# Softmax numerators of the first block in SBUF, and their low fp16 half on GpSimd

## The chip, the cores and the metric

The kernel runs on one core of a Trainium2 chip. The metric is the device time of one launch, in microseconds (us). The core has five engines that work through queues of their own, in order: TensorE (PE, with PEld for its weight loads), VectorE (DVE), ScalarE (ACT), GpSimd (POOL) and SyncE (SP, which here only issues DMAs).

## What is computed

The first block is two layers over 512 latent tokens and, in the first layer, 256 context tokens as well. Each layer adds three gated branches: a Fourier branch, a neighbourhood attention (NA, 8 heads of 64) and a latent attention (MLA, 8 heads of 96), then a layer norm and a gated feed-forward. A second block follows (sliding-window and forgetting attention, a recurrent unit, 16 experts). The attentions of the first block all have this form:

```
for each layer l in (0, 1):                   # "last" in layer 1: no context queries
    NA :  P = exp(q k^T / 8 + bias - max);  y = (P v) / sum(P)     # 256 window keys + 256 context keys
    MLA:  P = exp(q k^T / sqrt(96) - max);  y = (P v) / sum(P)     # 768 keys
    context queries (layer 0 only): the same over the 256 context keys
```

Matmuls are to be float32-accurate, so every operand is kept as a pair of fp16 numbers, a high half and a low half (the low half is the value less the high half), and each product is three matmuls: high by high, high by low, low by high.

## The kernel before

**Units.** The attentions run as units, one for a tile of 128 queries. An NA unit (`na_unit`) takes a pair of heads at 512 keys each, so a tile of numerators of 128 x 1024; a context unit (`ctx_unit`) a pair of heads at 256 keys, 128 x 512; an MLA unit (`mla_head`) one head at 768 keys, 128 x 768. Layer 0 has four pairs of 4 NA units and 2 context units, then four pairs of 8 MLA units and 2 context units; layer 1 the same without the context units. So there are 32 units of 128 x 1024, 64 of 128 x 768 and 16 of 128 x 512, in four stages: NA and MLA of layer 0, NA and MLA of layer 1.

**Steps of a unit.** The scores S are six or twelve matmuls into one of three PSUM buffers of 128 x 1024 (`big()`, pool `ps2`), which every projection of the kernel uses too. DVE takes the maximum of each row (L904, or L871 and L874) and scales it (L906, L877); ACT writes exp(S) back over S in PSUM, with its row sums (L908, L881). Then `turn_rows`: ACT copies the numerators to fp16 (L766, the high half), DVE subtracts that from the numerators in PSUM (L767, the low half), both into a tile p16 with two buffers, and two DMAs on SP's queue turn the halves into ph (L769; three buffers). PE multiplies ph by v (L152, L154, L156: the first two use the high half of ph, L156 the low half), DVE divides by the sums (L786, L788), PE transposes (L794), and ACT and DVE make the pair of fp16 halves (L161, L162).

**Order.** `pipeline` emits the stages of consecutive units overlapped: the scores of unit u, `turn_rows` of u - 1, the product with v of u - 4 (u - 2 in NA). Between them come "fills": the projections that make q, k and v of the next pair (`na_prep`, `mla_prep`), and the gated projections of the branch before (`branch`), whose weights are loaded by SP into a staging tile and split by ACT (L124) and DVE (L129, both inputs in SBUF) into a pair in pool `w16`. The framework's scheduler then fixes one order of instructions per engine, by a model of its own.

**GpSimd** has little to do in these stages: it adds the gated branches up (L638), scales the bias of NA (L843), and issues the DMAs of the shifted v, the bias and of part of k (L839 to L842, L1011). All of its inputs here lie in SBUF.

Of the kernel before, what the change touches and what calls it, by code (L numbers as in the profile page):

```python
# [9 lines left out]
F32 = mybir.dt.float32  # L10
# [47 lines left out]
class Net:  # L58
    def __init__(self, ctx, tc, I, out):
# [6 lines left out]
        # staging, hi/lo and modulation weight buffers  # L66
        self.wst = ent(tc.tile_pool(name="wst", bufs=4))
        self.w16 = ent(tc.tile_pool(name="w16", bufs=8))
# [6 lines left out]
    def open_x(self):  # L75
        """Residual tiles; their pool sits on the other side of SBUF until close_x()."""
# [44 lines left out]
    # ---------------------------------------------------------------- helpers  # L121
# [23 lines left out]
    def mm3(self, outs, lhs, rhs, first=True, last=True):  # L145
        """outs[j] += lhs[k].T @ rhs[j][k]; every operand is a (hi, lo) pair."""
# [11 lines left out]
    def hilo(self, dst, src, scale):  # L158
        """dst[:, 0/1] (fp16) = hi/lo of scale * src."""
# [4 lines left out]
    def rsqrt(self, v, shape, pool, tag):  # L164
        """1/sqrt(v) for v > 0, float32-accurate; returns a new tile."""
# [11 lines left out]
    def token_rsqrt(self, sqs, nt, scale, eps, pool):  # L177
        """1/sqrt(scale * (mean over 256 features of sqs) + eps) of every token: a function that puts it on all
        partitions, in PSUM."""
# [19 lines left out]
    def dense(self, w, act, kts, chunks, m, first=True, last=True, outs=None):  # L199
        """w: (p, 2, k, c); act: list of (p, 2, k, T) per chunk."""  # L200
# [4 lines left out]
    def dense_early(self, ws, ctx, outs):  # L205
        """dense over all tokens with each of the weights, a chunk of tokens at a time."""
# [5 lines left out]
    # ------------------------------------------------------------ modulation  # L212
# [16 lines left out]
    def modvec(self, w_ap, cols, bias, mod):  # L229
        """Generator of small steps: mod (p, 48, len(cols)) = columns of silu(c) @ w_mod + b_mod, feature  # L230
        128 * index + p."""
        nc = self.nc
        for g in range(3):
            row = self.sm.tile([128, 512], F32, tag="mrow", name="mrow", bufs=1)
            for kt in range(KD):
                # the first third, whose steps follow one another, adds up in PSUM
# [19 lines left out]
    def modvec_sums(self, w_ap, cols, bias, mod, new, keep={}):  # L256
        """As modvec, with the sums over kt on the vector engine."""
# [54 lines left out]
    def pump(self, n=1):  # L312
        """Emit up to n steps of the background work."""
        while n and self.bg is not None:
            if next(self.bg, self) is self:
                self.bg = None
            n -= 1
# [5 lines left out]
    def affine(self, name, g, b, mod, i_shift, i_scale, nm):  # L323
        """(g, b) of a norm followed by x * (1 + scale) + shift, times AS: (p, 8, nm) each."""
# [29 lines left out]
    # ------------------------------------------------------------ layer norms  # L354
# [34 lines left out]
    def stats(self, x, t0, n, g=None, gb=None):  # L389
        """PSUM tile, on all partitions: mean over features of x in [:, :n], of x^2 in [:, n:2n]; with g and  # L390
        gb, of x * gb and (x * g)^2."""
# [18 lines left out]
    def ln_chunk(self, x, t0, n, apply, between=None):  # L410
        """In place: x[:, :, t0:t0+n] <- (x - mean) * rstd, then apply()."""
# [1824 lines left out]
```

## Time and profile before

| | before |
|---|---|
| time, median of 3 runs | 2865.58 us (2861.57, 2865.58, 2868.97) |
| span of the profiled execution | 2860.5 us |
| PE busy | 2571.4 us, 90% |
| DVE busy | 1787.7 us, 62% |
| ACT busy | 1130.4 us, 40% |
| POOL busy | 277.3 us, 10% |

The span runs from the first to the last instruction; what lies around it is some us more (the three times are 1.1 to 8.5 us above the span, 5.1 us at the median). The page has no time of the profiled execution itself, only this span. The shares are averages over stages with different limits, so the four attention stages have to be read one by one: 126 to 335 us (NA, layer 0), 400 to 635 us (MLA, layer 0), 1423 to 1584 us (NA, layer 1) and 1632 to 1814 us (MLA, layer 1).

### The profile page before, as it was taken

Reading aid. Unit: us, or ns where it says so; the run is one execution under the profiler, and the core shown is the slowest. Engines: PE = TensorE matmul, PEld = TensorE weight load, DVE = VectorE, ACT = ScalarE, POOL = GpSimd, SP = SyncE. Lnnn points to the kernel's source line nnn. Section 1 sums busy time; section 2 is a strip of 40 time slices with the busy share of each in tenths; the row PEclk is TensorE's granted clock in tenths of the full one; section 3 lists DMA queues with packets and bytes.
Section 4 is the critical chain, followed back from the end, with each engine's and each line's share of the span. In section 5 each row is a group of like instructions: output and inputs, shape, how many; then the busy total and the mean of one; then the engine's idle time right before and its main releaser. Section 6 shows DMA issues by size and latency. Waiting matters only on the chain. (4 is left out here: it accounts for less than half of the span.)

```text
span 2860.5 us, 45500 instructions
## 1 busy us (share of the span) xinstructions
PE 2571.4 (90%) x18514; PEld 1537.5 (54%) x18514; DVE 1787.7 (62%) x3041; ACT 1130.4 (40%) x1876; POOL 277.3 (10%) x229
## 2 busy tenths in 40 slices
PE   6999988899999999999998888999999887886784
PEld 4766555556675555556665444466444444543342
DVE  7555586653375656364655767547565477879895
ACT  4444344443342122123644355434222244544562
POOL 4100000011000000000000000100000000013552
PEclk9999899999999999999998989999999998877997
DMA  9366546683034535251455267525665603646883
GB/s 313 94 150 134 114 112 135 138 189 98 23 94 128 148 97 150 76 158 39 132 130 127 70 120 144 134 60 161 200 185 160 174 16 74 138 133 217 273 286 115
DMA packets 561674, 389.13 MB, mean 136 GB/s; under 512 B 229644, under 2 KB 524108, under 8 KB 561200
## 3 DMA queue, kind: packets, MB, share of 16 engines
q1 hardware_dynamic: 547568, 344.75, 46.0%
q0 software_dynamic: 13024, 38.24, 4.2%
q8 instruction: 147, 2.41, 0.3%
q10 hardware_dynamic: 864, 3.15, 0.3%
q14 instruction: 71, 0.58, 0.1%
HBM read 316.29 MB, written 23.62 MB: 119 GB/s over the span
## 5 line engine op out<-in xcount | busy, mean ns | idle before, releaser
L152 PE MATMUL ps<-aL,w 128*128 128x512 f16 (+1 forms) x1504 | 541.1, 361 | 16.1 <-DVE p L767 10.6
L154 PE MATMUL ps<-aL,w 128*128 128x512 f16 (+1 forms) x1504 | 541.4, 360 | 1.1 <-DVE aL L444 1.0
L156 PE MATMUL ps<-aL,w 128*128 128x512 f16 (+1 forms) x1504 | 540.6, 360 | 0.0
L124 ACT ACTIVATE w<-wst 128x1024 f16<-128x1024 f32 (+2 forms) x333 | 340.1, 1023 | 461.0 <-PE ps L156 412.6
L129 DVE SCALAR_TENSOR_TENSOR w<-wst,w 128x1024 f16<-128x1024 f32 (+2 forms) x326 | 400.4, 1232 | 161.3 <-ACT w L124 159.3
L152 PEld LDWEIGHTS <-w 128*128 128x128 f16 (+1 forms) x3276 | 323.4, 99 | 286.9 <-issue 49.6
L156 PEld LDWEIGHTS <-w 128*128 128x128 f16 (+1 forms) x3276 | 324.2, 99 | 255.7 <-issue 40.1
L154 PEld LDWEIGHTS <-w 128*128 128x128 f16 (+1 forms) x3276 | 324.9, 99 | 236.4 <-issue 25.9
L154 PE MATMUL ps<-aC,w 128*128 128x256 f16 (+1 forms) x720 | 196.4, 273 | 0.8 <-DVE aC L444 0.7
L152 PE MATMUL ps<-aC,w 128*128 128x256 f16 (+1 forms) x720 | 196.1, 273 | 1.1 <-ACT aC L443 1.1
L156 PE MATMUL ps<-aC,w 128*128 128x256 f16 (+1 forms) x720 | 196.3, 273 | 0.0
L278 DVE SCALAR_TENSOR_TENSOR mv<-wmod,csilu,mv 128x1024 f32<-128x1024 f32 x126 | 158.4, 1280 | 35.0 <-DMA wmod<-in_w_mod 34.6
L767 DVE TENSOR_TENSOR p<-ps,p 128x768 f16<-128x768 f32 (+2 forms) x126 | 125.9, 1001 | 76.9 <-ACT p L766 76.2
L766 ACT ACTIVATE p<-ps 128x768 f16<-128x768 f32 (+2 forms) x126 | 106.5, 848 | 31.1 <-DMA ph<-p 28.7
L152 PE MATMUL ps<-h,w 128*128 128x512 f16 (+1 forms) x384 | 111.4, 344 | 0.8 <-ACT h L1117 0.8
L154 PE MATMUL ps<-h,w 128*128 128x512 f16 (+1 forms) x384 | 111.3, 344 | 0.7 <-DVE h L1118 0.7
L156 PE MATMUL ps<-h,w 128*128 128x512 f16 (+1 forms) x384 | 111.3, 344 | 0.0
L638 POOL TENSOR_TENSOR acc<-acc,gt 128x768 f32<-128x768 f32 (+1 forms) x32 | 54.3, 1696 | 505.8 <-DVE gt L637 443.0
L908 ACT ACTIVATE ps<-ps,nm 128x768 f32<-128x768 f32 (+1 forms) x96 | 70.1, 730 | 76.0 <-DVE nm L906 70.1
L1113 ACT ACTIVATE ft<-ps 128x768 f32<-128x768 f32 (+1 forms) x44 | 30.9, 702 | 173.4 <-PE ps L156 173.3
L152 PEld LDWEIGHTS <-ph 128*128 128x128 f16 x800 | 78.2, 104 | 37.3 <-DMA ph<-p 23.1
L904 DVE TENSOR_REDUCE mx<-ps 128x1 f32<-128x768 f32 (+1 forms) x80 | 71.6, 898 | 42.2 <-PE ps L156 41.4
(688 smaller groups left out, 5171.1 us busy)
## 6 DMA issues: line engine op xcount, KB each, us to landing
wmod<-in_w_mod SPq DMA_DIRECT2D x144, 512.0 KB, 4.5
wst<-in_w_in SPq DMA_DIRECT2D x101, 512.0 KB, 4.2
wst<-in_w_ffn_gate SPq DMA_DIRECT2D x44, 512.0 KB, 4.1
wst<-in_w_ffn_up SPq DMA_DIRECT2D x44, 512.0 KB, 3.9
wst<-in_w_ffn_down SPq DMA_DIRECT2D x44, 512.0 KB, 4.6
wst<-in_w_branch SPq DMA_DIRECT2D x24, 512.0 KB, 3.6
wst<-in_w_out SPq DMA_DIRECT2D x24, 512.0 KB, 3.7
wst<-in_w_gate SPq DMA_DIRECT2D x38, 256.0 KB, 4.3
```

Of the source, the lines that this page charges most:

```text
L124: nc.scalar.activation(w[:, HI], src, AF.Copy, scale=WS)
L129: nc.vector.scalar_tensor_tensor(w[:, LO], src, WS, w[:, HI], ALU.mult, ALU.subtract)
L152: mm(o, lhs[k][HI], rhs[j][k][HI], start=s, stop=False)
L154: mm(o, lhs[k][HI], rhs[j][k][LO], start=False, stop=False)
L156: self.last_mm = mm(o, lhs[k][LO], rhs[j][k][HI], start=False, stop=e)
L278: nc.vector.scalar_tensor_tensor(a, st, self.cs[:, kt, c:c + 1], a, ALU.mult, ALU.add)
L638: nc.gpsimd.tensor_tensor(self.acc[:, kt + 1], self.acc[:, kt + 1], t[:, :T], op=ALU.add)
L766: nc.scalar.activation(hi, P, AF.Copy)
L767: nc.vector.tensor_tensor(lo, P, hi, op=ALU.subtract)
L904: nc.vector.tensor_reduce(mx[:, :nh], Sv, AX.X, ALU.max)
L908: nc.scalar.activation(P[:, h], Sv[:, h], AF.Exp, scale=SC, bias=nm[:, h:h + 1], accum_out=sums[:, h:h + 1])
L1113: nc.scalar.activation(t, pg[:, :T], AF.Tanh, scale=0.5 * INV)
```

## The change

In the three kinds of units the exponential writes into a new SBUF tile p32 (two buffers) and no longer over the scores in PSUM. `turn_rows` then reads p32 twice: ACT makes the high half, and GpSimd, which is now passed as the engine, the low half. The sliding-window and forgetting attentions of the second block still call `turn_rows` without an engine and keep DVE. To make room for p32, pool `w16` has six buffers and not eight; in the expert stage a second pool gets six and not four, so both together stay at twelve there, and the experts and the last two tiles of the output projection's weights are handed out over the two pools accordingly. Beside this only comments go. Line numbers of the code behind `turn_rows` move by up to seven (L767 becomes L768, L638 stays, L908 becomes L913).

```diff
-        self.w16 = ent(tc.tile_pool(name="w16", bufs=8))
+        self.w16 = ent(tc.tile_pool(name="w16", bufs=6))
...
-    def turn_rows(self, pool, P, nh, ntile):
+    def turn_rows(self, pool, P, nh, ntile, eng=None):
+        eng = eng or nc.vector
...
-        nc.vector.tensor_tensor(lo, P, hi, op=ALU.subtract)
+        eng.tensor_tensor(lo, P, hi, op=ALU.subtract)
...
+    def rows32(self, pool, nh, n):
+        return pool.tile([128, nh * n], F32, tag="p32", name="p32", bufs=2).rearrange("p (h c) -> p h c", h=nh)
...
-        P = Sv
+        P = self.rows32(ap, 2, 512)
...
-        ph = self.turn_rows(ap, P, 2, 4)
+        ph = self.turn_rows(ap, P, 2, 4, self.nc.gpsimd)
...
-        P = S[:, None, :NT]
-        self.softmax_rows(ap, P, NT, SC, sums[:, h:h + 1], P)
+        P = self.rows32(ap, 1, NT)
+        self.softmax_rows(ap, S[:, None, :NT], NT, SC, sums[:, h:h + 1], P)
...
-        ph = self.turn_rows(ap, P, 1, 6)
+        ph = self.turn_rows(ap, P, 1, 6, self.nc.gpsimd)
...
+        spare = lambda: self.half[1].tile([128, 2, 1056], F16, tag="w16", name="w16")[:, :, None, :D]
...
-                tc.tile_pool(name="wxh", bufs=4, reuse_waits="tile") as x16:
+                tc.tile_pool(name="wxh", bufs=6, reuse_waits="tile") as x16:
```

The context units change as the NA units do, at 256 keys. Since a scheduler fixes the order, two places of it are shown.

DVE before, in MLA of layer 0, where the second pair's q is made (p16 with ps2 as its source is the low half of a unit, mx and nm the maximum and its scaled copy, krn and qh the rotation of q, w16 a split of weights):

```order
L906 TENSOR_SCALAR nm_5424<-mx_5422 128x1
L162 SCALAR_TENSOR_TENSOR yT_4087<-ps1_5493,yT_4087 128x128
L129 SCALAR_TENSOR_TENSOR w16_6421<-wst_6419,w16_6421 128x1024
L904 TENSOR_REDUCE mx_5482<-ps2_5475 128x1
L1058 TENSOR_TENSOR ps2_5453<-ps2_5453,ctab_91 32x512
L906 TENSOR_SCALAR nm_5484<-mx_5482 128x1
L767 TENSOR_TENSOR p16_5487<-ps2_5415,p16_5487 128x768
L1059 SCALAR_TENSOR_TENSOR krn_4093<-ps2_5453,ctab_91 32x512
```

DVE of the changed kernel at the same place (mx_5520 is the maximum that was mx_5482):

```order
L909 TENSOR_REDUCE mx_5520<-ps2_5512 128x1
L1063 TENSOR_TENSOR ps2_5490<-ps2_5490,ctab_91 32x512
L911 TENSOR_SCALAR nm_5522<-mx_5520 128x1
L129 SCALAR_TENSOR_TENSOR w16_6249<-wst_6247,w16_6249 128x1024
L1064 SCALAR_TENSOR_TENSOR krn_4117<-ps2_5490,ctab_91 32x512
L791 RECIPROCAL ri_5867<-sums_5450 128x2
```

The low half is gone from DVE's queue; the split of weights that stood ahead of the maximum now stands behind its scaled copy.

POOL before, in MLA of layer 0, from the second pair on (acc is the sum of the branches, kh the DMAs of a later pair's k):

```order
L638 TENSOR_TENSOR acc_454<-acc_454,gt_5572 128x768
L638 TENSOR_TENSOR acc_454<-acc_454,gt_5787 128x768
L1011 DMA kh_6003<-krn_4093 32x1536
L1011 DMA kh_6007<-krn_4093 32x1536
L638 TENSOR_TENSOR acc_454<-acc_454,gt_6258 128x768
```

POOL of the changed kernel at the same place:

```order
L768 TENSOR_TENSOR p16_5626<-p32_5519,p16_5626 128x768
L768 TENSOR_TENSOR p16_5694<-p32_5620,p16_5694 128x768
L638 TENSOR_TENSOR acc_454<-acc_454,gt_5610 128x768
L768 TENSOR_TENSOR p16_5746<-p32_5688,p16_5746 128x768
L768 TENSOR_TENSOR p16_5843<-p32_5740,p16_5843 128x768
L768 TENSOR_TENSOR p16_5913<-p32_5837,p16_5913 128x768
L638 TENSOR_TENSOR acc_454<-acc_454,gt_5828 128x768
L1016 DMA kh_6048<-krn_4117 32x1536
L768 TENSOR_TENSOR p16_5966<-p32_5906,p16_5966 128x512
```

Between two sums of branches there are now two to five low halves, and some low halves stand behind a sum or behind a DMA of kh.

## Rows read from the trace of the kernel before

**Rows 1.** Stages: us; busy PE, PEld, DVE, ACT, POOL; granted clock, DMA share, GB/s
```profile
126.00:335.00 209.00, 201.85 (x1962) 131.22 (x1960) 107.81 (x247) 89.06 (x180) 9.82 (x12) 0.95 0.63 136
...
400.00:635.00 235.00, 202.65 (x1771) 124.77 (x1770) 153.12 (x278) 114.09 (x216) 18.18 (x14) 0.95 0.70 144
...
1423.00:1584.00 161.00, 152.57 (x1476) 95.60 (x1475) 86.21 (x196) 70.76 (x135) 9.86 (x12) 0.95 0.59 132
...
1632.00:1814.00 182.00, 153.02 (x1210) 82.50 (x1209) 122.71 (x207) 96.64 (x163) 12.03 (x12) 0.90 0.66 124
```

**Rows 2.** PE's waits, 400 to 635 us: releaser, total us, times, longest
```profile
PE ps L152 <- DVE p L767: 11.5, 10, 3.6
...
PE ps L156 <- DMA ph<-p: 3.7, 8, 0.6
PE ps L152 <- DVE kh L162: 3.6, 2, 1.8
...
PE ps L152 <- DVE vm L162: 2.2, 2, 1.4
```

**Rows 3.** PE's waits, 1632 to 1814 us
```profile
PE ps L152 <- DVE p L767: 7.9, 4, 2.9
PE ps L156 <- DMA ph<-p: 5.9, 6, 2.2
...
PE ps L152 <- DVE vm L162: 2.8, 2, 1.8
...
PE ps L152 <- DVE kh L162: 2.2, 1, 2.2
```

**Rows 4.** PE's waits, 126 to 335 us
```profile
PE ps L156 <- DMA ph<-p: 2.4, 1, 2.4
...
PE ps L152 <- DVE p L767: 1.0, 1, 1.0
```

**Rows 5.** PE's waits, 1423 to 1584 us
```profile
PE ps L152 <- DVE p L767: 2.9, 2, 2.1
PE ps L156 <- DMA ph<-p: 1.0, 2, 0.6
```

**Rows 6.** Timeline around one stall of PE: start, us, instruction, idle before
```profile
475.42 0.86 ACT L908 ACTIVATE ps<-ps,nm 128x768 f32<-128x768 f32 x1
...
476.77 0.79 ACT L766 ACTIVATE p<-ps 128x768 f16<-128x768 f32 x1
...
478.60 0.96 DVE L767 TENSOR_TENSOR p<-ps,p 128x768 f16<-128x768 f32 x1
...
479.61 0.39 PE L152 MATMUL ps<-aL,w 128*128 128x512 f16 x1 [1.94 <-DVE p L767]
```

**Rows 7.** Groups by shape, DVE and ACT: count, busy us, mean ns, idle before
```profile
L129 DVE SCALAR_TENSOR_TENSOR w<-wst,w 128x1024 f16<-128x1024 f32 x306 | 388.3, 1273 | 141.3 <-ACT w L124 139.3
...
L767 DVE TENSOR_TENSOR p<-ps,p 128x768 f16<-128x768 f32 x66 | 62.8, 955 | 46.9 <-ACT p L766 46.4
...
L767 DVE TENSOR_TENSOR p<-ps,p 128x1024 f16<-128x1024 f32 x41 | 50.0, 1220 | 20.7 <-ACT p L766 20.6
...
L627 ACT ACTIVATE gt<-ps 128x768 f32<-128x768 f32 x24 | 19.4, 810 | 72.4 <-PE ps L156 72.4
```

**Rows 8.** The same view of POOL
```profile
L638 POOL TENSOR_TENSOR acc<-acc,gt 128x768 f32<-128x768 f32 x16 | 33.2, 2073 | 289.7 <-DVE gt L637 289.7
...
L127 POOL TENSOR_TENSOR w<-wst,w 128x1024 f16<-128x1024 f32 x7 | 16.2, 2319 | 0.6
```

**Rows 9.** Timeline of a DVE instruction beside one of POOL
```profile
449.52 1.80 POOL L638 TENSOR_TENSOR acc<-acc,gt 128x768 f32<-128x768 f32 x1 [14.20 <-DVE gt L637]
...
449.96 2.45 DVE L129 SCALAR_TENSOR_TENSOR w<-wst,w 128x1024 f16<-128x1024 f32 x1
```

**Rows 10.** The transposing DMAs (L769), from issue to landing
```profile
DMA to landing us min/median/max: 2.4/3.4/10.4
```

**Rows 11.** ACT's waits, 400 to 635 us
```profile
ACT p L766 <- DMA ph<-p: 14.6, 8, 4.3
```

More of the change, by code (lines that the diff above doesn't have):

```diff
@@ L923, in ctx_unit @@
         sums = ap.tile([128, 2], F32, tag="sums", name="sums", bufs=4)
-        P = Sv
+        P = self.rows32(ap, 2, 256)
         self.softmax_rows(ap, Sv, 256, SC, sums, P)
         yield
-        ph = self.turn_rows(ap, P, 2, 2)
+        ph = self.turn_rows(ap, P, 2, 2, self.nc.gpsimd)
         yield
@@ L1331, in out_proj @@
         self.bcast_rows(lp, op)
-        wo = [self.load_w(self.I["w_out_2"][128 * k:128 * k + 128, None, :], 1, D)[:, :, 0] for k in range(KD)]
+        spare = lambda: self.half[1].tile([128, 2, 1056], F16, tag="w16", name="w16")[:, :, None, :D]
+        wo = [self.load_w(self.I["w_out_2"][128 * k:128 * k + 128, None, :], 1, D, spare() if k >= 6 else None)[:, :, 0]
+              for k in range(KD)]
         aT = self.aT = self.xp.tile([128, 2, KD, NL], F16, tag="aL", name="a3")
@@ L1932, in expert_weights @@
             self.nblk += n > 0
-            out.append(self.split_expert(b, self.load_expert(e, b, st), self.half[n % 2 == 0 and b < 4]))
+            out.append(self.split_expert(b, self.load_expert(e, b, st), self.half[n % 2 == 0]))
         return out
@@ L2043, in experts @@
             hT[n] = self.turn(ep, hgs[n])
-            W[n] = self.expert_weights(n, n) if n else W0[:4] + [self.split_expert(b, W0[b], self.w16) for b in (4, 5)]
+            W[n] = self.expert_weights(n, n) if n else W0[:4] + [self.split_expert(b, W0[b], self.half[1]) for b in (4, 5)]
         next(steps)
```

## The prediction

> **What bounds the kernel now.** First the busy times by stage. In the four stages that the change touches PE is busy 201.9 of 209 us, 202.7 of 235, 152.6 of 161 and 153.0 of 182 [rows 1]: it is idle for 7.1, 32.4, 8.4 and 29.0 us, 76.9 us in all. No other engine comes near its share (DVE 153 of 235 and 123 of 182 at most), so what the change can give lies in those 76.9 us, nearly all of it in the two MLA stages, and in the granted clock, which is 0.90 to 0.95 there.
>
> Then what ended PE's waits, stage by stage. "PE L152 <- DVE L767" means that PE wanted a PSUM buffer for new scores or a new projection, and the buffer came free when DVE had made the low half of an earlier unit: 11.5, 7.9, 1.0 and 2.9 us [rows 2 to 5], together 23.3 us in 17 waits. Waits for k and v of the next pair (kh and vm, DVE's L162) are 3.6 + 2.2 us and 2.2 + 2.8 us [rows 2, 3], 10.8 us in 8 waits. L156 is the one matmul of a product that reads the low half of ph, so "L156 <- DMA ph" tells how often the low half was what came last: 3.7, 5.9, 2.4 and 1.0 us [rows 2 to 5], 13.0 us in 17 waits.
>
> Last the timeline at one stall, to see how long a buffer is held after its exponential. The exponential starts at 475.42 and ends at 476.28, the high half is made from 476.77, the low half from 478.60 to 479.56, and at 479.61 PE goes on after 1.94 us of waiting [rows 6]. The buffer was held for 3.3 us after the exponential, longer than the stall.
>
> **Part A, the buffer of the scores comes free after the exponential.** In the changed kernel nothing reads PSUM after it. In rows 6 that is 3.3 us earlier, more than the 1.94 us of the wait, and all 17 waits are of 3.6 us or less. If they go whole, 23.3 us are gained. But PE then stands earlier at the next thing: the maximum and the exponential of the newest unit, or kh and vm, which it waits for already. I take two thirds, 15.5 us; the bounds are 23.3 us and a third, 8 us.
>
> **Part B, DVE loses 112 subtractions.** 32 of 1.220 us, 64 of 0.955 us [rows 7], and 16 of 128 x 512, whose price I put at 0.7 us by the two others: 39 + 61 + 11 = 111 us of DVE's time. DVE is not the bound, so only what stands behind them counts: the 8 waits for kh and vm would each come up to 0.955 us earlier, were a low half just ahead in DVE's queue. I take half of that, 8 x 0.48 = 3.8 us; the bounds are 0 and 7.6 us.
>
> **Part C, the low half takes longer on GpSimd.** The trace has no GpSimd subtraction of 768; the nearest row is L638 with two float32 inputs, 1.80 us when nothing is in its way [rows 9], 2.07 us in the mean [rows 8]. For 1024 the row is L127, the same operation with the same types, 2.32 us [rows 8]. So a low half comes 0.85 us (768) or 1.10 us (1024) later, if it starts as early. It may start earlier, as POOL's queue is nearly empty (9.8 to 18.2 us busy in a stage [rows 1]). What PE feels is bounded by the waits of L156: 14 in MLA x 0.85 + 3 in NA x 1.10 = 15.2 us if each gets longer by the full amount, 0 if the earlier start makes up for it. Within one run of waits the first shifts the others too, so I take half, 7.6 us lost.
>
> **Part D, DVE and GpSimd hold each other up.** At 449.52 POOL starts an L638 of 1.80 us; at 449.96 DVE starts a split L129, both of whose inputs are in SBUF, and it takes 2.45 us instead of 1.27 in the mean [rows 7, 9]. It ended 1.09 us after POOL did: it had waited. The old low half read PSUM and one SBUF tile; the new one is just such a two-input instruction on POOL, 112 times. In MLA of layer 0 they fill 32 x 1.80 us and 8 x 1.2 us (two thirds of it, for 512 keys) = 67 of 235 us, 29%, so about 3 in 10 of the splits meet one and wait half of it, 0.27 us for each split. By the code there are 6 splits for a pair in NA and 5 in MLA, for 8 pairs each: 88, so 24 us of DVE's time, against the 111 that it was spared. On PE's path I take 2 us, between 0 and a third of it, 8 us.
>
> The Trainium skill (GPSIMD Engine Reference, Key points) says the same: GpSimd shares its SBUF interfaces with VectorE and contends with DVE instructions that have two SBUF inputs. The trace agrees (2.45 us beside 1.27), and this rule speaks against the change; it is the mechanism of the first rival.
>
> **Part E, ACT.** The exponential now writes SBUF. L908 with PSUM as its target takes 0.86 us [rows 6]; a tanh of the same 128 x 768 from PSUM to SBUF takes 0.81 us [rows 7]. So I cost it at nothing; the bound is 0.1 us on each of 160 exponentials, on an engine that is busy 114 of 235 us, and ACT's own slack covers it. The high half reads SBUF instead of PSUM; the same cover hides that. The Trainium skill (ScalarE: Activation LUTs, Step-by-step: what each stage is for) holds PSUM to be the faster target of ScalarE. The two rows here do not show it; by that rule the exponentials would be dearer by an amount that it doesn't give.
>
> **Part F, six weight buffers and the experts.** PE's order outside the four stages is nearly the same, a pair of an attention stage needs 5 or 6 weights, and the expert stage has twelve buffers as before. I take 0; the bound is two splits late by 1.27 us each at a stage's start, 2.5 us. The p32 tiles (two) are free again when the low half is made: about 0.9 + 0.8 + 1.8 us of work against 2 x 5.9 us (235 us for 40 units), so they bind nothing.
>
> **Part G, the clock.** Granted shares of 0.95, 0.95, 0.95 and 0.90 [rows 1] mean that PE had 1.2 instead of 2.4 GHz in 10% to 20% of the time. That is 209 x 0.05 + 235 x 0.05 + 161 x 0.05 + 182 x 0.10 = 48 us of full-speed work at most, and in a good part of it PE was waiting anyway. With less idle time some of it returns; I take a twentieth, 2.3 us, between 0 and an eighth, 6 us.
>
> **The sum.** -15.5 - 3.8 + 7.6 + 2 + 0 + 0 - 2.3 = -12.0 us. The profiled span is 2860.5 us, the median 2865.6; the 5.1 us between them lie outside of the span and do not change. So 2848.5 us of span and 2853.6 us of time, 0.42% faster. A measurement of this kernel tells about 0.3%, 8.6 us, from no change.
>
> **Rivals.** *The port and the late low half eat the gain.* Part C in full (15.2) and part D at its upper bound (8), with A, B and G as above, give -15.5 - 3.8 + 15.2 + 8 - 2.3 = +1.6: 2867.2 us, no difference. For it speaks rows 9, against it that PE's order has been rebuilt with GpSimd's low halves in it, and that products with v come four units after their scores in MLA.
>
> *Slower: GpSimd's queue becomes a chain.* In the new order sums of branches stand between low halves, and low halves behind a DMA of kh. A low half that waits there keeps its p16 buffer; ACT, which works in order, then stops at the next high half, as it does already for 14.6 us in one stage [rows 11], and the exponentials behind it keep the scores' buffers again. A p16 buffer is now held for 0.8 (high) + 0.96 (low [rows 6]) + 3.4 us (landing [rows 10]), 5.2 us and what SP's queue adds, of 11.8 us for two units. With 1.8 us for the low half it is 6.0 us. So it decides from 5.8 us of lateness on. If at each of the 16 sums of branches in the MLA stages the low half behind is held up past that point and PE loses the 1.80 us of the sum, 16 x 1.80 = 29 us are lost against the 12 of the forecast: 2882.6 us. Against it: POOL would be busy for a third of a stage only.
>
> *The buffer was not the limit.* PE stops a moment later at the exponential or at kh instead, and A gives a quarter, 5.8 us: -5.8 - 3.8 + 7.6 + 2 = 0.0, 2865.6 us. For it: PE's waits have many releasers, and ACT and DVE stand within a few us of each other. Against it: the release comes 3.3 us earlier where 1.94 were missing.
>
> **How the numbers follow.** Forecast 0.50 (2839 to 2857, by the bounds of A and C), the port 0.22 (2857 to 2872), not the limit 0.14 (2860 to 2870), the chain 0.14 (2874 to 2890). The predicted time is the forecast's, 2853.6 us. The range takes the forecast and the two cases of no difference, 2838 to 2871 us, and leaves out the chain and a few hundredths at the ends. Faster by over 0.3% (under 2857.0): 0.50. Within 0.3%: 0.36. Slower: 0.14.
>
> **What would show it.** A right: PE's waits on the low half are gone from the four stages, and what stands in their place (waits on the exponential) is under 10 us. B: the waits on kh and vm get shorter. C and D: the low half takes 1.8 to 2.1 us for 768, waits of L156 on ph grow by up to 15 us, and L129 gets longer in the mean than 1.27 us. E: the exponential stays under 0.95 us. G: the granted clock of MLA in layer 1 rises above 0.90. The prediction is wrong if PE's idle time in the four stages is not about 10 us less than 76.9, if ACT's waits for ph grow well beyond 14.6 us in MLA, or if a stage outside of the four moves by more than 3 us.

## The result, and the profile after

| | before | after |
|---|---|---|
| time, median | 2864.94 us (4 runs, 2861.57 to 2868.97) | 2826.32 us (4 runs, 2824.64 to 2831.72) |
| span of the profiled execution | 2860.5 us | 2825.6 us |
| PE / DVE / ACT / POOL busy | 2571.4 / 1787.7 / 1130.4 / 277.3 us | 2558.2 / 1702.7 / 1126.4 / 453.4 us |

The ratio is 0.9871, with a 95% interval of 0.9852 to 0.9890. The change makes the kernel 1.3% faster, three times as much as predicted (2853.6 us), and the time lies below the range (2838 to 2871 us). One execution of experiment 7 took 5582 us, twice the others, and is left out of its figures.

The windows after, cut at the same matmuls as those of [rows 1] (the four attention stages, in their order, then the last 213 us of the expert stage): stretch in us, its length, busy time of PE, PEld, DVE, ACT and POOL with the number of instructions, granted clock (the share of PE's full clock that it was given), DMA share, GB/s.

```profile
122.00:331.00 209.00, 199.32 (x1961) 129.86 (x1960) 87.45 (x223) 87.32 (x180) 52.90 (x36) 0.96 0.64 137
397.50:624.30 226.80, 203.47 (x1771) 125.22 (x1769) 121.83 (x238) 113.78 (x216) 80.30 (x54) 0.94 0.72 149
1411.40:1568.20 156.80, 150.40 (x1476) 94.03 (x1475) 77.93 (x178) 71.01 (x135) 43.89 (x28) 0.97 0.61 136
1615.90:1782.80 166.90, 147.25 (x1210) 82.04 (x1209) 101.12 (x176) 97.10 (x163) 66.67 (x44) 0.92 0.68 132
...
2612.90:2825.60 212.70, 148.47 (x760) 72.44 (x759) 164.78 (x205) 109.19 (x132) 89.80 (x59) 0.89 0.68 233
```

Against [rows 1] the four stages took 209, 235, 161 and 182 us before, 787 in all; now they take 209.0, 226.8, 156.8 and 166.9, 759.5 in all, 27.5 us less. Two things make that up. PE's idle time (length less busy time, summed) fell from 76.9 to 59.1 us, by 17.8. And the same matmuls kept PE busy for 700.4 us instead of 710.1: 9.7 us less, most of it in the last stage, where the granted clock rose from 0.90 to 0.92; in MLA of layer 0 it fell from 0.95 to 0.94, with 9.0 us less idle time. These are profiles of one execution each, and 23 executions of the kernel before on one chip took 2854.8 to 2870.9 us, at mean granted clocks of 0.942 to 0.948. So parts of a few us are not certain. The other 7.4 of the span's 34.9 us lie outside of the four stages.

PE's waits after, in MLA of layer 0 (the first lines) and of layer 1: releaser (what ended the wait), total us, times, longest.

```profile
PE ps L152 <- ACT p L913: 4.4, 4, 1.8
PE ps L152 <- DVE nm L911: 3.1, 2, 1.9
PE ps L245 <- DVE yT L162: 3.0, 2, 1.5
PE ps L245 <- issue: 2.7, 2, 1.4
PE ps L156 <- DMA ph<-p: 2.7, 3, 1.8
...
PE ps L152 <- DVE vm L162: 1.4, 1, 1.4
```

```profile
PE ps L152 <- DMA ph<-p: 5.8, 3, 3.1
PE ps L156 <- DMA ph<-p: 3.5, 3, 2.3
PE ps L799 <- DVE y L793: 2.8, 1, 2.8
PE ps L152 <- ACT p L913: 2.8, 3, 1.4
...
PE ps L152 <- DVE vm L162: 0.9, 1, 0.9
PE ps L152 <- DVE kh L162: 0.2, 1, 0.2
```

The 23.3 us on the low half [rows 2 to 5] are gone. Where PE now waits for a scores' buffer, the exponential is the last reader: 4.4 + 2.8 us here and 0.5 in NA of layer 0, 7.7 us. The waits on kh and vm, 10.8 us in [rows 2, 3], are 2.5 us. The waits of L156 on ph, where a late low half would show, are 2.7 + 3.5 here and 4.2 and 2.4 in NA, 12.8 us against 13.0.

One unit in the timeline after, at the place in MLA of layer 0 that answers to [rows 6] (start, us, instruction, idle before):

```profile
473.05 0.90 ACT L913 ACTIVATE p<-ps,nm 128x768 f32<-128x768 f32 x1 [1.44 <-DVE nm L911]
...
474.07 0.84 ACT L767 ACTIVATE p<-p 128x768 f16<-128x768 f32 x1
...
475.05 1.64 POOL L768 TENSOR_TENSOR p<-p,p 128x768 f16<-128x768 f32 x1 [4.23 <-ACT p L767]
```

The buffer is free at 473.95, with the exponential. The low half is ready at 476.69, 1.78 us after the high half; in [rows 6] it was 2.00 us after it, since DVE came to it 1.04 us late and GpSimd comes at once (0.14 us).

Groups by shape after: count, busy us, mean ns, idle before. The last line is the half of k that is read out of the projection in PSUM.

```profile
L768 POOL TENSOR_TENSOR p<-p,p 128x768 f16<-128x768 f32 x64 | 106.1, 1658 | 236.0 <-ACT p L767 221.0 <-issue 10.7 <-DMA ph<-p 2.2
L768 POOL TENSOR_TENSOR p<-p,p 128x1024 f16<-128x1024 f32 x32 | 68.0, 2127 | 157.0 <-ACT p L767 127.8 <-issue 29.2
L129 DVE SCALAR_TENSOR_TENSOR w<-wst,w 128x1024 f16<-128x1024 f32 x304 | 395.8, 1306 | 174.0 <-ACT w L124 172.3
L913 ACT ACTIVATE p<-ps,nm 128x768 f32<-128x768 f32 x64 | 57.3, 895 | 46.5 <-DVE nm L911 43.0 <-DVE ri L791 2.5 <-POOL p L768 0.9
...
L162 DVE SCALAR_TENSOR_TENSOR kh<-ps,kh 64x768 f16<-64x768 f32 x16 | 15.2, 953 | 7.2 <-ACT kh L161 6.9
```

GpSimd's idle time ahead of its low halves ended with the high half in 221.0 of 236.0 us: it is ready when the high half comes. The exponential into SBUF takes 895 ns; into PSUM it took 0.86 us in [rows 6] and 871 ns in the mean.

### The profile page after: what moved, and what is told of

Read it like the earlier page. It is cut to its first block, busy times and chain, and to the rows that moved or that the text cites. A ratio compares the mean times of both kernels' runs of the same rounds, so it can differ in the third digit from the quotient of the medians.

```text
span 2825.6 us, 45658 instructions
## 1 busy us (share of the span) xinstructions
PE 2558.2 (91%) x18514; PEld 1531.4 (54%) x18514; DVE 1702.7 (60%) x2929; ACT 1126.4 (40%) x1876; POOL 453.4 (16%) x341
## 3 DMA queue, kind: packets, MB, share of 16 engines
q8 instruction: 147, 2.41, 0.3%
## 5 line engine op out<-in xcount | busy, mean ns | idle before, releaser
L156 PE MATMUL ps<-aL,w 128*128 128x512 f16 (+1 forms) x1504 | 538.7, 359 | 0.0
L129 DVE SCALAR_TENSOR_TENSOR w<-wst,w 128x1024 f16<-128x1024 f32 (+2 forms) x324 | 411.5, 1274 | 191.9 <-ACT w L124 190.1
L156 PEld LDWEIGHTS <-w 128*128 128x128 f16 (+1 forms) x3276 | 324.0, 99 | 251.2 <-issue 33.7
L768 POOL TENSOR_TENSOR p<-p,p 128x768 f16<-128x768 f32 (+2 forms) x112 | 192.6, 1720 | 449.3 <-ACT p L767 400.4
L156 PE MATMUL ps<-aC,w 128*128 128x256 f16 (+1 forms) x720 | 196.5, 273 | 0.0
L156 PE MATMUL ps<-h,w 128*128 128x512 f16 (+1 forms) x384 | 111.1, 344 | 0.0
L767 ACT ACTIVATE p<-p 128x768 f16<-128x768 f32 (+2 forms) x112 | 97.7, 873 | 32.8 <-DMA ph<-p 27.5
L913 ACT ACTIVATE p<-ps,nm 128x768 f32<-128x768 f32 (+1 forms) x96 | 72.1, 753 | 63.8 <-DVE nm L911 59.6
```

What stands on the lines that cost most here:

```text
L129: nc.vector.scalar_tensor_tensor(w[:, LO], src, WS, w[:, HI], ALU.mult, ALU.subtract)
L156: self.last_mm = mm(o, lhs[k][LO], rhs[j][k][HI], start=False, stop=e)
L767: nc.scalar.activation(hi, P, AF.Copy)
L768: eng.tensor_tensor(lo, P, hi, op=ALU.subtract)
L913: nc.scalar.activation(P[:, h], Sv[:, h], AF.Exp, scale=SC, bias=nm[:, h:h + 1], accum_out=sums[:, h:h + 1])
```

## The experiments

The first theory was that the release of the scores' buffer is the whole gain, and that GpSimd is only the place where the low half went. Its rivals were that the relief of DVE, or the new buffer pools, make the gain. Later a further question came up: how little slack GpSimd's low half has. The figures of all kernels are in the table behind the experiments. Each ratio is against the kernel before, run on the same chip in turns with it; each kernel gets its own order from the scheduler.

**1. The pools alone.** The kernel before with six buffers in `w16`, six in the second pool, and the weights handed out as in the changed kernel; numerators stay in PSUM.

```diff
-        self.w16 = ent(tc.tile_pool(name="w16", bufs=8))
+        self.w16 = ent(tc.tile_pool(name="w16", bufs=6))
...
-                tc.tile_pool(name="wxh", bufs=4, reuse_waits="tile") as x16:
+                tc.tile_pool(name="wxh", bufs=6, reuse_waits="tile") as x16:
```

> The kernel before with nothing but the new pools: six weight buffers, six in the second pool, and the experts' and the output projection's weights handed out as in the changed kernel. The exponential writes PSUM and DVE makes the low half as before. Outside the four attention stages the changed kernel moved by -5.3 us in the first Fourier stage, +3.5 us in the hybrid stage and -6.8 us in the expert loop, some -8 us in all. Theory 'pools': these come from the pools and the order that goes with them, so this kernel takes about 2857 us (2864.9 before), with PE's idle time in the four stages at 77 us as before. Theory of the prediction (part F, nothing): 2865 us, and the 8 us came from elsewhere.

Measured: 2859.23 us, ratio 0.9988 (0.9977 to 1.0000), about 3 us. PE still waits for the low half in MLA of layer 0, as in [rows 2], but the Fourier stage ahead of the attentions, 83.7 us long before, takes 78.3 as in the changed kernel. Those two rows, of this kernel (the wait first, then the window):

```profile
PE ps L152 <- DVE p L767: 11.6, 10, 3.9
```

```profile
43.70:122.00 78.30, 74.73 (x717) 59.55 (x717) 54.40 (x122) 43.59 (x93) 32.98 (x30) 0.97 0.50 149
```

The pools move stages that the numerators don't touch; in all they are worth a tenth of the gain (by the interval, nothing to two tenths).

**2. SBUF, but DVE makes the low half.** The changed kernel without GpSimd, in all three kinds of units.

```diff
-        ph = self.turn_rows(ap, P, 1, 6, self.nc.gpsimd)
+        ph = self.turn_rows(ap, P, 1, 6)
```

> The changed kernel with one part undone: the numerators go to SBUF, but DVE makes the low half. The four stages gained 27 us in the changed kernel. Theory 'buffer': that the scores' buffer is free after the exponential is what counts; two thirds or more of the 27 us stay, the time is 2839 us or less. Theory 'DVE': what counts is that 111 us of work left DVE; here they are back, the four stages gain 5 us or less, the time is about 2850 us (with the 8 us outside the stages).

Measured: 2827.19 us, ratio 0.9880 (0.9859 to 0.9901), the same as the changed kernel. The waits of PE in MLA of layer 0, of this kernel:

```profile
PE ps L152 <- ACT p L913: 8.1, 6, 3.1
...
PE ps L152 <- DVE nm L911: 2.4, 1, 2.4
...
PE ps L152 <- DVE vm L162: 0.2, 1, 0.2
```

With DVE as busy as before, the waits on the low half are gone, and those on kh and vm too (2.3 us over the four stages, from 10.8). So neither needed GpSimd. Nor is it that SBUF is read faster than PSUM: the high half takes 841 ns (809 before) and DVE's low half 986 ns (955 before) for 128x768.

**3. The buffer held until the high half.** The changed kernel, with a one-column DVE instruction that reads the scores and the high half, so that the buffer comes free later: 2.1 us after the exponential in the mean of the MLA units, where it was 2.6 to 3.0 us (means by layer) before the change.

```diff
         eng.tensor_tensor(lo, P, hi, op=ALU.subtract)
+        if held is not None:
+            mark = pool.tile([128, 1], F32, tag="mark", name="mark", bufs=2)
+            nc.vector.tensor_tensor(mark, held, p16[:, HI, 0:1], op=ALU.add)
```

> The changed kernel with the other part undone: GpSimd makes the low half from SBUF, but an added DVE instruction of one column reads the scores and the high half, so that the scores' buffer stays taken until the high half is made and DVE comes to it, some 2 of the 3.3 us for which it was held before. Theory 'buffer': of the 27 us of the four stages no more than 12 stay, the time is 2840 us or more. Theory 'DVE': DVE is as free as in the changed kernel but for 112 instructions of about 0.1 us, 22 us or more stay, the time is 2832 us or less.

Measured: 2839.9 us, ratio 0.9914 (0.9896 to 0.9933): a third of the gain is lost. PE's waits for a buffer are back under the name of the mark, first in MLA of layer 0, then of layer 1:

```profile
PE ps L152 <- DVE mark L771: 8.5, 8, 2.8
...
PE ps L152 <- DVE vm L162: 2.4, 2, 1.3
```

```profile
PE ps L152 <- DVE mark L771: 10.0, 5, 3.4
...
PE ps L152 <- DVE kh L162: 3.0, 2, 1.9
```

Over the four stages they are 20.0 us, and the waits on kh and vm come back with them, to 8.7 us. So the moment of release pays, and kh and vm are tied to it. But the time lies at the edge of what the theory 'buffer' expected: with the buffer held for three quarters of the old time, about three quarters of these waits are back, yet the four stages keep 16.2 of the 27.5 us, more than the 12 that it allowed. PE's busy time stayed at 701.3 us and the stages outside kept their gain; what holds these two is not shown.

**4. Each low half twice.** The changed kernel, GpSimd's subtraction repeated into the same tile, so the low half is late by about its own length.

```diff
         eng.tensor_tensor(lo, P, hi, op=ALU.subtract)
+        if eng is not nc.vector:
+            eng.tensor_tensor(lo, P, hi, op=ALU.subtract)
```

> The changed kernel with each of GpSimd's 112 subtractions done twice (the second writes the same values), so a low half is ready 1.66 us (768) or 2.13 us (1024) later and POOL is busy about 190 us more. By the prediction's part C PE would feel it through the waits for the low half of ph: up to 17 x 1.7 = 29 us, half of it 15 us, so about 2841 us. Theory 'slack': a low half is used units later, and p16 has several us to spare, so the time rises by under 5 us, to 2831 us at most. Theory 'chain' (the slower rival): GpSimd is close to binding already, and the time rises by over 30 us.

Measured: 2867.32 us, ratio 1.0011 (0.9999 to 1.0023): the whole gain is gone, 40 us, as the theory 'chain' had it. In MLA the low half is ready 2.1 us (layer 0) and 2.3 us (layer 1) later than in the changed kernel. PE's waits in MLA of layer 1, of this kernel:

```profile
PE ps L156 <- DMA ph<-p: 7.9, 5, 3.2
PE ps L152 <- DMA ph<-p: 6.8, 3, 3.7
PE ps L152 <- ACT p L915: 4.7, 4, 2.7
```

Waits on ph are 41.0 us in the four stages (27.5 in the changed kernel), those on the exponential 13.9 (7.7).

**5. GpSimd as busy, but the low half on time.** As 4, with the repetition into a tile that nobody reads.

```diff
+        if eng is not nc.vector:
+            junk = pool.tile([128, n], F16, tag="junk", name="junk", bufs=1)
+            eng.tensor_tensor(junk.rearrange(pat, **kw), P, hi, op=ALU.subtract)
```

> The changed kernel with GpSimd's subtraction done a second time into a tile that nobody reads: GpSimd is as busy as in the run that made each low half twice (2867 us, 40 us over the changed kernel), but the low half is ready after the first. 'Lateness' (those 40 us came from the low half coming 1.7 to 2.1 us later itself): a loss of under 10 us, 2826 to 2836 us, ratio 0.987 to 0.990. 'Queue' (they came from what a busy GpSimd does to the rest: low halves and sums of branches behind it in its queue, buffers held, DVE held up): a loss of 25 us or more, 2851 us and above, ratio over 0.9955.

Measured: 2842.83 us, ratio 0.9926 (0.9900 to 0.9952), 16 us over the changed kernel. That lies between the two expectations: of the 40 us of experiment 4, 24 are the lateness of each low half itself, and 16 what a doubly busy GpSimd does to the rest (its queue, buffers held, DVE held up; not separated here). One part of the rest shows in ACT's idle time ahead of the exponentials, here those of MLA:

```profile
L916 ACT ACTIVATE p<-ps,nm 128x768 f32<-128x768 f32 x64 | 57.5, 898 | 60.1 <-DVE nm L914 44.5 <-POOL junk L771 11.5 <-DVE ri L794 2.8
```

The exponential waits for a p32 buffer that GpSimd still reads, 24.3 us in all shapes together. In experiment 4 it is 25.4 us, in the changed kernel 2.8.

**6. Both engines make the low half, DVE's is used.** Experiment 2, with GpSimd doing the same subtraction into a tile that nobody reads.

```diff
-        eng.tensor_tensor(lo, P, hi, op=ALU.subtract)
+        nc.vector.tensor_tensor(lo, P, hi, op=ALU.subtract)
+        if eng is not None:
+            junk = pool.tile([128, n], F16, tag="junk", name="junk", bufs=1)
+            eng.tensor_tensor(junk.rearrange(pat, **kw), P, hi, op=ALU.subtract)
```

> The kernel in which DVE makes the low half from p32 (ratio 0.988, 2827 us), and beside it GpSimd does the same subtraction into a tile that nobody reads; the outputs are right. So nothing waits for GpSimd's result, and only its hold-up of DVE (part D) and its hold on p32 and p16 are added. 'Both worthless' (DVE's relief and GpSimd's hold-ups are each about nothing): 2824 to 2830 us, ratio 0.987 to 0.989, and L129's mean rises to about 1.31 us as in the changed kernel without harm. 'They cancel' (moving the low half spares 4 us or more by part B, and the hold-ups take as much): 2831 to 2836 us, ratio 0.9895 to 0.991.

Measured: 2856.4 us, ratio 0.9971 (0.9953 to 0.9989): 26 us worse than experiment 2 by the ratios, far more than either theory allowed.

**7. Both engines make it, GpSimd's is used.** The mirror of 6: the changed kernel, with DVE repeating the subtraction into a tile that nobody reads.

```diff
+        if eng is not nc.vector:
+            junk = pool.tile([128, n], F16, tag="junk", name="junk", bufs=1)
+            nc.vector.tensor_tensor(junk.rearrange(pat, **kw), P, hi, op=ALU.subtract)
```

> The changed kernel with the 112 subtractions given back to DVE as well, into a tile that nobody reads: only DVE's relief (part B) is undone. 'Part B as forecast': 3.8 us or more lost, 2830 to 2834 us, ratio 0.989 to 0.991. 'DVE's time is worth nothing here': 2824 to 2829 us, ratio 0.9865 to 0.988.

Measured: 2853.26 us, ratio 0.9965 (0.9950 to 0.9980), 27 us worse than the changed kernel; again neither theory. The groups of 6 (first fence) and 7 (second) show what the two have in common:

```profile
L770 POOL TENSOR_TENSOR junk<-p,p 128x768 f16<-128x768 f32 x64 | 141.6, 2212 | 223.1 <-ACT p L766 222.6
...
L767 DVE TENSOR_TENSOR p<-p,p 128x768 f16<-128x768 f32 x64 | 75.7, 1184 | 43.1 <-ACT p L766 25.5 <-issue 13.4 <-POOL junk L770 3.6
```

```profile
L768 POOL TENSOR_TENSOR p<-p,p 128x768 f16<-128x768 f32 x64 | 139.8, 2186 | 222.7 <-ACT p L767 168.8 <-DVE qh L162 14.8 <-issue 10.1
...
L771 DVE TENSOR_TENSOR junk<-p,p 128x768 f16<-128x768 f32 x64 | 74.2, 1160 | 47.8 <-ACT p L767 47.4
```

Both subtractions wait for the same high half and mostly start together, and both means are longer: 2.2 us on GpSimd instead of 1.66, 1.16 to 1.18 on DVE instead of 0.99 (experiment 2). But each mean mixes two cases, and in a single pair one of the two is held until the other has ended. A pair of each kind, of 6 (start, us, instruction):

```profile
475.67 1.64 POOL L770 TENSOR_TENSOR junk<-p,p 128x768 f16<-128x768 f32 x1 [2.42 <-ACT p L766]
476.35 1.78 DVE L767 TENSOR_TENSOR p<-p,p 128x768 f16<-128x768 f32 x1
...
484.38 0.96 DVE L767 TENSOR_TENSOR p<-p,p 128x768 f16<-128x768 f32 x1 [1.85 <-issue]
...
484.43 2.41 POOL L770 TENSOR_TENSOR junk<-p,p 128x768 f16<-128x768 f32 x1 [7.11 <-ACT p L766]
```

In the first, GpSimd takes its usual time and DVE ends 0.82 us after it; in the second, DVE takes its usual time and GpSimd ends 1.50 us after it. Of 64 subtractions of this shape on GpSimd, 11 are of the first kind (DVE ends 0.81 to 0.89 us later), 49 of the second (GpSimd ends 1.50 to 1.58 us later), and 4 meet none of DVE's; the counts of 7 are the same. (The time of the held one includes its wait: 1.78 and 2.41 us in the rows above.) Two explanations were left for the 27 us: DVE's extra work as such, or this meeting.

**8. DVE's extra work without the meeting.** The changed kernel, with DVE taking the maximum over p32: as long as the subtraction, with one input.

```diff
+        if eng is not nc.vector:
+            mark = pool.tile([128, 2], F32, tag="mark", name="mark", bufs=2)
+            nc.vector.tensor_reduce(mark[:, :a], P, AX.X, ALU.max)
```

> The changed kernel with a further DVE instruction for each of the 112 tiles: the maximum over p32, into a mark that nobody reads. It has one input only, and as long as the maximum over PSUM it takes about 0.96 us for 768 and 0.68 for 512, so DVE gets back about as much work as the subtractions were. The run in which DVE repeated the subtraction itself (two inputs in SBUF, at the same moment as GpSimd's) lost 28 us. 'DVE's time' (those 28 us are the 111 us of DVE's work): 2848 to 2858 us, ratio 0.995 to 0.998. 'Meeting' (they came from two instructions with two SBUF inputs each that start together and hold each other up): 2826 to 2834 us, ratio 0.987 to 0.990.

Measured: 2828.12 us, ratio 0.9867 (0.9845 to 0.9889), no loss. The groups of this kernel:

```profile
L768 POOL TENSOR_TENSOR p<-p,p 128x768 f16<-128x768 f32 x64 | 106.4, 1663 | 235.0 <-ACT p L767 222.8 <-issue 7.9 <-DMA ph<-p 3.0
...
L771 DVE TENSOR_REDUCE mark<-p 128x1 f32<-128x768 f32 x64 | 60.8, 951 | 21.9 <-ACT p L916 21.1
```

DVE got back 111 us of work (60.8, 39.0 and 10.9 us in three shapes), and neither it nor GpSimd took longer for each tile. So DVE's time as such is worth nothing here, and the meeting is what costs. This is not the same meeting with one input fewer, though: the maximum waits for the exponential alone (the releaser in its row) and mostly runs before the low half. Of GpSimd's 64 subtractions 23 ran beside one in part, and none of these maxima was held (936 to 954 ns).

**9. GpSimd beside DVE, without a hold on buffers.** Experiment 2, with GpSimd subtracting the row sums from a constant into a tile that nobody reads.

```diff
+        if eng is not None:
+            own = self.ident[:, None, :].to_broadcast([128, n // 128, 128])
+            eng.tensor_tensor(self.junk[:, :n].rearrange("p (j c) -> p j c", c=128), own,
+                              sums[:, :, None].to_broadcast([128, n // 128, 128]), op=ALU.subtract)
```

> Low half on DVE from p32 (alone 0.988, 2827 us), and GpSimd does a subtraction of the same size for each tile from a constant and the row sums into a tile that nobody reads: it holds neither p32 nor p16, so only the hold-up of DVE is left of the run with the doubled subtraction (2856 us). 'Hold-ups' (GpSimd's running beside DVE costs the 28 us): 2848 to 2858 us, ratio 0.995 to 0.998. 'Buffers' (the 28 us came from p32 and p16 that GpSimd held longer): 2826 to 2834 us, ratio 0.987 to 0.990.

Measured: 2838.57 us, ratio 0.9909 (0.9893 to 0.9926), 8 us worse than experiment 2 by the ratios (11 by the medians), hardly clear of noise and between the two expectations. The groups of this kernel:

```profile
L771 POOL TENSOR_TENSOR junk<-ident,sums 128x768 f16<-128x768 f32 x64 | 98.6, 1541 | 253.4 <-ACT p L917 251.8 <-ACT yT L162 1.5
L768 DVE TENSOR_TENSOR p<-p,p 128x768 f16<-128x768 f32 x64 | 86.7, 1356 | 36.7 <-ACT p L767 36.4
```

DVE's low half takes 1.36 us instead of 0.99, with no data shared; in 42 of the 64 units it ends 0.81 to 0.93 us after GpSimd's instruction. So the hold-up without shared buffers costs some 8 us, where experiment 6 lost 26. It is a smaller hold-up, too: DVE is busy for 470.9 us in the four stages in experiment 2, 504.1 here and 521.2 in experiment 6. Against experiment 2 DVE's low halves grew by 28 us in both; other instructions grew in 6 above all (L129 takes 1262 ns in experiment 2, 1285 here, 1323 in 6, though 1322 cost nothing in 8). Whether the rest is those, or the hold on p32 and p16, is not settled.

**10. A mix.** Low half on DVE, but on GpSimd in the odd heads of MLA.

```diff
-        ph = self.turn_rows(ap, P, 1, 6, self.nc.gpsimd)
+        ph = self.turn_rows(ap, P, 1, 6, self.nc.gpsimd if h else None)
```

> The numerators in SBUF as in the changed kernel, the low half on DVE, but on GpSimd for the odd heads of MLA alone (32 of 112 units): DVE is spared where its queue is fullest, and GpSimd never has two low halves in a row. If DVE's relief and GpSimd's lateness are each worth a few us, this takes the better of both: 2820 to 2824 us, ratio 0.985 to 0.9865. If neither matters: 2825 to 2829 us, ratio 0.987 to 0.988.

Measured: 2825.45 us, ratio 0.9873 (0.9848 to 0.9899): the same as the changed kernel.

**11. The mix, with halves in tiles of their own.** Three buffers for the high half, two for the low one.

```diff
-        p16 = pool.tile([128, 2, n], F16, tag="p16", name="p16", bufs=2)
+        p16 = [pool.tile([128, n], F16, tag="p16" + t, name="p16" + t, bufs=b) for t, b in (("h", 3), ("l", 2))]
```

> The kernel with GpSimd's low half in the odd heads of MLA alone (2825 us), with the two halves in tiles of their own, three buffers for the high half and two for the low one; everything is computed. ACT waits 15.7 us in MLA of layer 0 and 8 us in layer 1 for the landing of the halves before it may write a high half. If these waits delay the exponentials that PE stands at (5.9 us in MLA of layer 0): 2812 to 2821 us, ratio 0.983 to 0.986. If ACT's slack covers them: 2822 to 2829 us, ratio 0.9865 to 0.988.

Measured: 2822.06 us, ratio 0.9867 (0.9845 to 0.9889), the edge of the second expectation. It can't be told from the changed kernel (0.9871), so no version here beats it.

The four stages together, of each kernel: their time, PE's idle and busy time (from the windows), and PE's waits by releaser, summed over the stages. "Scores' buffer" is the releaser behind a read of the scores: low half, mark or exponential; "nm, y" are DVE's scaled maximum and the divided output.

| kernel | ratio | time | idle | busy | scores' buffer | kh, vm | ph | nm, y |
|---|---|---|---|---|---|---|---|---|
| before | 1 | 787.0 | 76.9 | 710.1 | 23.3 | 10.8 | 26.3 | 5.6 |
| after | 0.9871 | 759.5 | 59.1 | 700.4 | 7.7 | 2.5 | 27.5 | 9.4 |
| 1 pools | 0.9988 | 784.5 | 80.2 | 704.3 | 29.4 | 7.1 | 28.8 | 6.1 |
| 2 DVE's low half | 0.9880 | 750.7 | 57.7 | 693.0 | 10.7 | 2.3 | 22.8 | 8.9 |
| 3 held | 0.9914 | 770.8 | 69.5 | 701.3 | 20.0 | 8.7 | 26.7 | 4.7 |
| 4 twice | 1.0011 | 797.6 | 87.2 | 710.4 | 13.9 | 0 | 41.0 | 9.9 |
| 5 GpSimd busy | 0.9926 | 773.8 | 71.9 | 701.9 | 10.4 | 2.1 | 32.3 | 8.8 |
| 6 both, DVE's used | 0.9971 | 777.8 | 72.4 | 705.4 | 13.9 | 2.3 | 24.0 | 18.1 |
| 7 both, GpSimd's used | 0.9965 | 780.2 | 72.8 | 707.4 | 16.3 | 2.5 | 23.8 | 18.9 |
| 8 DVE, one input | 0.9867 | 758.6 | 59.6 | 699.0 | 9.7 | 2.2 | 23.3 | 6.3 |
| 9 GpSimd aside | 0.9909 | 766.5 | 62.4 | 704.1 | 8.2 | 2.6 | 21.7 | 13.4 |
| 10 mix | 0.9873 | 748.2 | 56.1 | 692.1 | 9.6 | 1.9 | 21.2 | 9.9 |
| 11 mix, own tiles | 0.9867 | 746.8 | 59.7 | 687.1 | 7.9 | 2.3 | 24.4 | 9.0 |

(For kh and vm only waits on DVE are counted.) In 6, 7 and 9 it is "nm, y" that grows, from 9 to 13 and 19 us: behind a subtraction that is held up stand, in DVE's queue, the maximum of the next unit and the division of an earlier one, and behind the maximum the exponential. In 4 and 5 it is ph.

## Why the prediction was too small

The order of causes was right: the buffer's early release is the main cause, and the rivals did not come about. "The buffer was not the limit" falls with experiments 2 and 3. "The port and the late low half eat the gain" and "GpSimd's queue becomes a chain" fall with the result; experiment 4 shows where their ground begins, at a low half that is about 2.1 to 2.3 us later still, and not at the 5.8 us of lateness that the prediction put it at. What failed were sizes, and in part B the cause. The largest step that failed is part C: it charged 7.6 us for a late low half, and PE's waits for it did not grow (12.8 us from 13.0). Nearly as large are part F, which put at nothing what became 7.4 us, and part G, which took 2.3 us where 9.7 came. Taken against the profiled spans, -12.0 us were forecast and -34.9 came. All parts at their favourable bounds would have given -36.9 us, 2828.7 us; the range stopped short of that because it moved A and C alone.

- **Part A** (-15.5) was right in its size: 23.3 us of waits became 7.7 on the exponential, a net 15.6, and the exponential is what was named as next in line. That it agrees to 0.1 us is luck: two thirds was a choice between bounds, and experiments 2 and 10, with the same early release, leave 10.7 and 9.6 us.
- **Part B** (-3.8) named the wrong cause. The waits on kh and vm lost 8.3 us, but with DVE's low half kept they vanish as well (experiment 2), they come back when the buffer is held (3), and 111 us of other work on DVE change nothing (8). L162 reads kh and vm out of projections in PSUM, in the same three buffers. Two of these waits in the timeline of PE before:

```profile
531.75 0.48 PE L152 MATMUL ps<-kh,qh 96*128 96x512 f16 x2 [1.41 <-DVE vm L162]
...
1639.40 0.61 PE L152 MATMUL ps<-cqn,w 128*128 128x512 f16 x1 [2.17 <-DVE kh L162]
```

Scores don't read vm, and the projection reads neither, so what they waited for was a buffer. (Two waits on kh stand ahead of scores, which do read kh; these may have been for either.) The step that failed was to count these 10.8 us apart from the 23.3. (By [rows 2, 3] they were 7 waits, not the 8 of the prediction; that moves the term by 0.5 us.)
- **Part C** (+7.6) never came. The low half takes 1.66 and 2.13 us, even less than the rows that it was bounded by [rows 8, 9], and in MLA it is ready about 0.5 to 0.7 us later in the mean than before (means over the units of each layer's stage, worked out from the trace: 1.70 and 1.86 us after the high half, from 1.22 and 1.19). But waits of L156 stayed at 12.8 us, from 13.0. A product with v comes four units after its scores in MLA; that slack, which was only named against the first rival, covers this lateness. It doesn't cover 2.1 to 2.3 us more (experiment 4: 40 us lost, 24 of them by lateness itself).
- **Part D** (+2) is of the right order: "nm, y" grew by 3.8 us. L129, the row that it was worked out from, rose only from 1273 to 1306 ns, 10 us over 304 splits, where 24 were forecast for the attentions alone. In MLA of layer 0 it took 1492 ns before and 1444 after. Splits have slack (experiment 8 lost nothing with 1322 ns); the price appears when the instruction held up stands ahead of a maximum (6, 7 and 9). One such is the scaling of the maximum itself, ahead of the exponential: 7 of the 48 scalings of 128x2 were held until 0.02 to 0.03 us after a low half of GpSimd ended, for up to 2.05 us and 6.2 us in sum. The other waits of PE, on yT above all (4.8 to 6.5 us), rose somewhat too. All idle time that A, B and C don't account for grew by 6.3 us.
- **Part E** (0) holds: 24 ns more for each exponential of 768 columns (871 to 895), under the bound of 0.1 us, and ACT's total fell.
- **Part F** (0, bound 2.5) was wrong in the trace: the Fourier stage gained 5.4 us (83.7 to 78.3) and the expert stretch 7.3 (220 to 212.7), while a hybrid stretch ahead of it lost 3. In sum 7.4 us lie outside of the four stages. Experiment 1 has the same 5.4 us of the Fourier stage without the numerators' change, and 3 us of time in all; in all kernels with the new pools the expert stretch is 211.9 to 216.8 us. So the step that put the pools at nothing failed. The sum is less sure: outside of the four stages these kernels' spans have 2064.5 to 2077.3 us, the kernel before 2073.5. That p32 binds nothing held for the changed kernel (2.8 us of ACT's waits), with little to spare (experiments 4 and 5).
- **Part G** (-2.3, bound 6) was too small: PE's busy time for the same matmuls fell by 9.7 us. By the working of the prediction, share by share, 48 us of full-speed work were lost to the clock before; now 209 x 0.04 + 226.8 x 0.06 + 156.8 x 0.03 + 166.9 x 0.08 = 40 us. Less waiting and a higher granted clock go together in MLA of layer 1: 29.0 us idle at 0.90 before, 19.7 at 0.92 after, 18.6 at 0.95 in experiment 2 and 26.1 at 0.90 when the buffer is held. But it isn't so everywhere. In MLA of layer 0 the clock fell with less idle time, and in experiment 1 PE's busy time over the four stages was 5.8 us below that of the kernel before, with 3.3 us more idle time, most of it in MLA of layer 0 (the row of [rows 1] has 202.65 us and 0.95):

```profile
396.50:629.70 233.20, 198.75 (x1770) 123.41 (x1769) 152.36 (x278) 113.10 (x216) 18.17 (x14) 0.98 0.67 140
```

No run here changes the clock alone, so what brought the 9.7 us stays open. The step that failed was to take a twentieth of the 48 us.

Set against the forecast: the waits on kh and vm give 4.5 us more, part C 7.8, the clock 7.4, the stages outside 7.4; part D and what stands beside it take 4.3 us more, and part A is off by 0.1. That is the 22.9 us between -12.0 and -34.9. The median fell by 38.6 us, 3.7 more than the span. In every execution that has both on record the time is 1.7 to 1.9 us above the span, so most of the 5.1 us that the prediction put outside of the span was the difference between executions.

Of what was to show it: the first condition for the prediction to be wrong held (idle time fell by 17.8 us, not by about 10), and so did the third (stages outside moved by more than 3 us). ACT's waits for ph in MLA of layer 0 are 15.8 us, from 14.6 [rows 11], so the second did not.

## What to carry to other kernels

When a PSUM buffer is passed round among several uses, count every wait for that pool as one group, whatever operation is named as the releaser: an earlier release gains on all of them. Moving work from an engine that is not the bound was worth nothing in itself here; what counted is whether the new place delays an instruction on the path, and by how much more than the slack of its consumer. Idle time is not all that a span is made of: PE's busy time for the same matmuls fell as well, by half as much as its idle time, and more than half of that fall is also in the trace of experiment 1, where idle time did not shrink. Before a mean duration is read as a slowdown of all, look at single instructions: in experiment 6 a mean of 1.18 us was 0.94 to 0.96 us in most subtractions and 1.2 to 2.4 us in the others.

## What the runs showed of the hardware

- Two subtractions with two SBUF inputs each, one on DVE and one on GpSimd, do not run side by side: in the 60 pairs of 128x768 that meet, in experiment 6 as in 7, the one that ends second does so 0.81 to 0.89 us (DVE) or 1.49 to 1.58 us (GpSimd) after the other, and the first keeps its usual time (medians of 0.96 and 1.64 us). The Trainium skill (GPSIMD Engine Reference, Key points) names contention for DVE instructions with two SBUF inputs; the runs agree, and show that GpSimd is held as well.
- A reduction on DVE with one SBUF input is not held where it does run beside GpSimd's subtraction: 936 to 954 ns (experiment 8). 111 us more of DVE's time cost nothing in this form; the same subtractions with two inputs cost 27 us (experiment 7).
- A small DVE instruction can be held as well: a scaling of 128x2 took up to 2.05 us beside a low half on GpSimd and 0.16 us otherwise; the 64 scalings of 128x1 all took 0.16 us or less.
- GpSimd is 1.74 times as slow as DVE for the low half (1658 against 955 ns for 128x768; DVE read the numerators from PSUM, and takes 986 ns from SBUF), and needed 0.14 us from the end of the high half to its start in the unit shown.
